# Forget-gate rows: repeated over the partitions by DMA from a scratch tensor in HBM, in place of GpSimd's broadcast

## The chip, the cores and the metric

The kernel runs on one core of one Trainium2 chip. The metric is the device time of one execution in microseconds (us), as a median of runs; less is better. The engines are TensorE (PE, matrix products; its weight loads are listed apart as PEld), VectorE (DVE), ScalarE (ACT), GpSimd (POOL) and SyncE (SP, which here only issues transfers). [...]

## The reference

Two layers of a decoder trunk work on 512 tokens of width 1024, in float32. Layer 0 splits its heads between differential attention (A) and forgetting attention (B), layer 1 uses dilated windows; each layer ends in a gated output projection and a per-layer embedding. What matters here is the forgetting attention. Each of its four heads has one gate logit per token, and the running sum of the logarithms of the gates' sigmoids is added to the scores, by query and by key:

```python
cum_logf = jnp.cumsum(jax.nn.log_sigmoid((f_logit + b_forget).astype(jnp.float32)), axis=1)
ob = fox_attention(qb, kb, vb.reshape(b, s_len, N_HEADS_B, HEAD_DIM), cum_logf)
...
s = jnp.einsum('bqhd,bkhd->bhqk', qb, k).astype(jnp.float32)
s = s + jnp.swapaxes(cqb, 1, 2)[..., None] - c_k[:, :, None, :]
pr = jax.nn.softmax(jnp.where(causal, s, -jnp.inf), axis=-1)
return jnp.einsum('bhqk,bkhd->bqhd', pr.astype(v.dtype), v)
```

With queries on the partitions and keys along the row, the term of the query is one number per partition, and the term of the key, c_k, is a row of 512 numbers that every one of the 128 partitions needs.

## The kernel before

The program is a list of chunks (add_chunk); a chunk is a block of weights of 1024 by 512 with its units, one unit per 128 tokens or 128 columns. Each float32 product is made of three products of split parts (mm3, L173 to L175): weights and activations are split into a high part (by ACT, L142 or L145) and a low part (by DVE, L143 or L146). Weights come in slices of 256 rows through three staging buffers named raw (prep_slices, L155, issued on SP); while one chunk runs, the slices of the next are loaded and split.

Attention is laid between the projection units: slot runs what was deferred, starts the attention steps that are due (attend), loads and splits weights, and then emits one projection unit. A head has four steps, one per 128 queries (head_steps): scores on PE, bias and row minimum on DVE (L445), exponential on ACT (L447), scaling by the reciprocal sum on POOL (L486), transposes on PE (L492) and the product with the values (L502), each stage a slot later. The order in which each engine then runs its instructions is set when the program is built, by a scheduler that simulates the engines; on the chip each engine and each queue follows its own list in order.

The forget gates are one unit of their own at the end of the second A chunk (f_unit). It puts the four heads' logits on partitions 0, 32, 64 and 96, takes the logarithms, and DVE's scan (L661) sums them along the tokens into the tile ck, of which these four partitions matter. Three slots later the columns of ck are transposed into cq, the term of the query. When a B head begins, POOL repeats that head's row of ck over all partitions, into a buffer of the pool t2, which has nine buffers in rotation:

```python
if i == 0:
    box["ck"] = t2()
    G.partition_broadcast(box["ck"], ck[32 * h:32 * h + 1, :])
bt = t2()
V.scalar_tensor_tensor(bt[:, :n], box["ck"][:, :n], cq[:, i, h:h + 1],
                       consts["causal"][:, off:512], op0=OP.subtract, op1=OP.add)
```

The four heads read it in their four steps (L465). After attention B come the gate units (z_units): DVE scales the projection (L705), ACT and DVE make the sigmoid (L688 to L692), DVE multiplies (L707), and POOL multiplies with the attention output (L709) before the result is split for the output projection (out_units, L719 to L738), whose first steps also build the mask of layer 1 on DVE (setup_c, L346 to L368).

Of the kernel before, what the change touches and what calls it, by code (L numbers as in the profile page):

```python
# [12 lines left out]
F32 = mybir.dt.float32  # L13
# [6 lines left out]
P = 128  # L20
# [5 lines left out]
BIG = 1e30  # L26
# [21 lines left out]
def trunk_kernel(  # L48
# [6 lines left out]
    nc = tc.nc  # L55
    V, A, G, T = nc.vector, nc.scalar, nc.gpsimd, nc.tensor

    cpool = ctx.enter_context(tc.tile_pool(name="cpool", bufs=1))
    sb = ctx.enter_context(tc.tile_pool(name="sb", bufs=1))
    psum = ctx.enter_context(tc.tile_pool(name="psum", bufs=1, space=bass.MemoryType.PSUM))  # L60

    cnt = [0]
# [28 lines left out]

    A.preload_act_table_set("natural_log_exp_and_others")

    # ---------------------------------------------------------------- inputs
    x2 = x[0]
    out2 = out[0]
    wie, wio = w_in_even[0], w_in_odd[0]
# [16 lines left out]
    rcol = const([P, NT], "rcol")  # L114
# [4 lines left out]
    gcols = const([P, 2, KS], "gcols")  # L119
    A.dma_start(out=gcols, in_=norm_g.rearrange("l (k q) -> q l k", q=P))  # L120

    # --------------------------------------------------------------- helpers
    def newton(y, ms, tmp):
        V.tensor_tensor(tmp, y, y, op=OP.mult)
        V.tensor_tensor(tmp, tmp, ms, op=OP.mult)
# [11 lines left out]
        return y  # L137

    def split(hi, lo, src, gain=None):
        """hi + lo = src (* gain, by partition), each exact in the tensor engine's one-pass type."""  # L140
        if gain is not None:
            A.activation(hi, src, AF.Copy, scale=gain)  # L142
            V.scalar_tensor_tensor(lo, src, gain, hi.bitcast(F32), op0=OP.mult, op1=OP.subtract)  # L143
            return
        A.activation(hi, src, AF.Copy)  # L145
        V.tensor_tensor(lo, src, hi.bitcast(F32), op=OP.subtract)  # L146
# [43 lines left out]
            mm3(ps, wh[:, k % 2, sl], wl[:, k % 2, sl], hi[:, k % 4, tok], lo[:, k % 4, tok],  # L190
                k == 0, k == KS - 1)

    # ---------------------------------------------------------- slot pipeline
    # A slot is one projection unit on the tensor engine plus what the deferred steps add to it.
    clock = [0]
    later = {}

# [13 lines left out]
            split(hi[:, :, t * P:(t + 1) * P], lo[:, :, t * P:(t + 1) * P], px)  # L211

    def row_scale(t0, t1):
        """rrow[:, token] = rcol of that token on every partition, by an exact product with the identity."""
        px = psX()
        for t in range(t0, t1):
            diag = t2((P, P))
            V.tensor_single_scalar(diag, ident, rcol[:, t:t + 1], op=OP.mult)
            T.matmul(px[:, t, :], onesd, diag, start=True, stop=True)
        A.activation(rrow[:, t0 * P:t1 * P].rearrange("p (t n) -> p t n", n=P), px[:, t0:t1, :], AF.Copy,  # L220
                     scale=float(P))

    def setup_a():
# [18 lines left out]
        for h in range(4):  # L242
            nc.sync.dma_start(out=bfc[32 * h:32 * h + 1, :], in_=b_forget[0:1, h:h + 1])

        # ------------------------------------------------------------- constants
        causal = const([P, 512], "causal")
        G.memset(causal, 0.0)
        G.affine_select(out=causal, in_=causal, pattern=[[-1, 512]], compare_op=OP.is_ge,
                        fill=BIG, base=384, channel_multiplier=1)
        # ------------------------------------------------------------ rope tables  # L250
        inv = np.exp((np.float32(-math.log(THETA)) * np.arange(16, dtype=np.float32)
                      / np.float32(16)).astype(np.float32)).astype(np.float32)
        posf = const([P, NT], "posf")
# [21 lines left out]
        for c in (c1, c2, c3):  # L275
            axpb(hsq, nn, -c, 0.0)
            gadd(ang, ang, hsq)
        # sin and cos of the reduced angle from those of its half, |half| <= pi / 2
        axpb(ang, ang, 0.5, 0.0)
        gmul(hsq, ang, ang)  # L280

        def series(first, last):
            """sum over n = first, first + 2, ..., last of (-1)^(n // 2) half^(n - first) / n!"""
            acc = t2((P, NT, 16))
            axpb(acc, hsq, (-1.0) ** (last // 2) / math.factorial(last), 0.0)
            for n in range(last - 2, first, -2):
                axpb(acc, acc, 1.0, (-1.0) ** (n // 2) / math.factorial(n))
                gmul(acc, acc, hsq)
            axpb(acc, acc, 1.0, 1.0)
            return acc  # L290
# [50 lines left out]
    def setup_c():  # L341
        causal = consts["causal"]
        biasc = sb.tile([P, 512], F32, tag="ckb", bufs=1, name="biasc")
        # d(p, c) = p + 384 - c ; multiplicity = [d <= 128] + [d % 4 == 0] + [d % 16 == 0]
        di = t2((P, 512), I32)
        G.iota(di, pattern=[[-1, 512]], base=384 + 512, channel_multiplier=1)  # L346
        mult = t2()
        tmi = t2((P, 512), I32)
        tmf = t2()
        V.tensor_single_scalar(tmi, di, 3, op=OP.bitwise_and)  # L350
        V.tensor_copy(tmf, tmi)
        V.tensor_single_scalar(mult, tmf, 0.0, op=OP.is_equal)
        tmi = t2((P, 512), I32)
        V.tensor_single_scalar(tmi, di, 15, op=OP.bitwise_and)
        tmf = t2()
        V.tensor_copy(tmf, tmi)
        V.scalar_tensor_tensor(mult, tmf, 0.0, mult, op0=OP.is_equal, op1=OP.add)
        tmf = t2()
        V.tensor_copy(tmf, di)
        V.scalar_tensor_tensor(mult, tmf, float(512 + 128), mult, op0=OP.is_le, op1=OP.add)  # L360
        # -ln(mult) for mult in 1..3, BIG where mult is 0 or d < 0
        V.tensor_single_scalar(biasc, mult, 2.0, op=OP.is_equal)
        V.tensor_single_scalar(biasc, biasc, -math.log(2.0), op=OP.mult)
        V.tensor_single_scalar(tmf, mult, 3.0, op=OP.is_equal)
        V.scalar_tensor_tensor(biasc, tmf, -math.log(3.0), biasc, op0=OP.mult, op1=OP.add)
        V.tensor_single_scalar(tmf, mult, 0.0, op=OP.is_equal)
        V.scalar_tensor_tensor(biasc, tmf, BIG, biasc, op0=OP.mult, op1=OP.add)
        V.tensor_tensor(biasc, biasc, causal, op=OP.add)  # L368

        consts["biasc"] = biasc  # L370

    # ------------------------------------------------------------- attention
    def qk_post(ps, qk, qk0, t, kind):
        """qk: hi and lo [P, 2(q/k), 2(head), 512], feature-major."""
        ng = 8 if kind == "a" else 4
        w = 512 // ng
        raw = t2()
# [5 lines left out]
        if kind != "b":  # L383
# [6 lines left out]
            for i in range(2):  # L390
# [6 lines left out]
                G.tensor_tensor(tt[:, 1, i, :, half:rot], v4[:, i, :, 0:half], tb(sg, half, rot), op=OP.mult)  # L397
                G.tensor_tensor(tt[:, 0, i, :, :], x12, tb(cg, 0, rot), op=OP.mult)
                G.tensor_tensor(x12, tt[:, 0, i, :, :], tt[:, 1, i, :, :], op=OP.add)
        # the projection still lacks the token's factor r: norm(r u) = r u (r^2 mean(u^2) + eps)^-1/2  # L400
        V.tensor_single_scalar(ss, ss, rcol2[:, t:t + 1], op=OP.mult)
        y = rstd_small(ss, 1.0 / w, ng)
        V.tensor_single_scalar(y, y, rcol[:, t:t + 1], op=OP.mult)
# [12 lines left out]

        defer(QLAG, finish)

    # steps waiting for their turn: (first slot, weight, first stage)
    queue = deque()  # L420
    credit = [0.0]

# [27 lines left out]
    def head_steps(kind, hh, qk, qk0, v, vcol, fin, first, extra=None):  # L450
        box = {}
# [4 lines left out]
        def step(i):  # L456
            n = P * (i + 1)
            off = 384 - P * i
            if kind == "b":
                ck, cq, h = extra  # L460
                if i == 0:
                    box["ck"] = t2()
                    G.partition_broadcast(box["ck"], ck[32 * h:32 * h + 1, :])
                bt = t2()
                V.scalar_tensor_tensor(bt[:, :n], box["ck"][:, :n], cq[:, i, h:h + 1],  # L465
                                       consts["causal"][:, off:512], op0=OP.subtract, op1=OP.add)
                bias = bt[:, :n]
            else:
                bias = consts["causal" if kind == "a" else "biasc"][:, off:512]
# [67 lines left out]
            cost = (i + 1) * (0.76 if kind == "a" else 0.55)  # L537
            queue.append((first[i], cost, lambda i=i: step(i)))

    # ------------------------------------------------------------- chunk code  # L540
    jobs = []

    def add_chunk(wap, ranges, nk, units, rate=0.0, layer=None):
# [90 lines left out]
    def f_unit(w):  # L634
        def u():
# [24 lines left out]
            ck = sb.tile([P, 512], F32, tag="ckb", bufs=1, name="ck")  # L660
            V.tensor_tensor_scan(ck, uu, xx, 0.0, op0=OP.mult, op1=OP.add)  # L661
            cq = const([P, NT, 4], "cq")
            st["ck"], st["cq"] = ck, cq

            def fin():
                px = psX()
# [16 lines left out]
        return hi, lo  # L683

    def sigmoid_of(z):
        """exp(log_sigmoid(z)), log_sigmoid(z) = min(z, 0) - ln(1 + exp(-|z|))."""
        e = t2()[:, :z.shape[-1]]
        A.activation(e, z, AF.Abs)  # L688
        A.activation(e, e, AF.Exp, scale=-1.0)
        A.activation(e, e, AF.Ln, bias=1.0)  # L690
        V.scalar_tensor_tensor(e, z, 0.0, e, op0=OP.min, op1=OP.subtract)  # L691
        A.activation(e, e, AF.Exp)  # L692
        return e
# [19 lines left out]
        return units  # L713

    def joined(act, j):
        """the float32 value that a pair of parts stands for"""
        hi, lo = act[j // 4]
        o = t2()
        G.tensor_tensor(o, hi[:, j % 4, :].bitcast(F32), lo[:, j % 4, :].bitcast(F32), op=OP.add)  # L719
        return o  # L720
# [47 lines left out]
        defer(1, tr)  # L768

    def ple(pp, w, t, a, b):  # L770
        """columns by tokens of the per-layer embedding (layer 0), tokens by columns (layer 1)"""
        wh, wl = w
        pT = st["pT"]
        sl = slice(t * P, (t + 1) * P)
        for k in range(2):
            ph, pl, vh, vl = pT[:, 0, k], pT[:, 1, k], wh[:, k], wl[:, k]
            if st["layer"] == 0:
                mm3(pp, vh[:, sl], vl[:, sl], ph[:, a:b], pl[:, a:b], k == 0, k == 1)
            else:
                mm3(pp, ph[:, sl], pl[:, sl], vh[:, a:b], vl[:, a:b], k == 0, k == 1)  # L780
# [5 lines left out]
    HALVES = ((0, 256), (256, 512))  # L786

    def gate0_units(c):
        """layer 0: feature-major, straight into the parts that layer 1 multiplies"""
        def units(w):  # L790
            wp_t, wp_f = prep_slices(w_ple[0], [(c * 512, 512)], 2)

# [62 lines left out]
        return e  # L855

    def gate1_units(c):
        """layer 1: token-major, straight into the rows of the result"""
        def units(w):
            wp_t, wp_f = prep_slices(w_ple[1], [(c * 512, 512)], 2)  # L860

# [30 lines left out]
    def qk_r(q0, k0, pr):  # L892
        return [(q0 + pr * 256, 256), (k0 + pr * 256, 256)]

    # layer 0
    RA = 2.7
    RB = 1.9
    RC = 2.2
# [37 lines left out]
            return units(w)  # L936
        return un

    # layer 1
    add_chunk(wio, [(2048, 512)], KS, reset(v_units("va")), layer=1)  # L940
    add_chunk(wio, qk_r(0, 1024, 0), KS, qk_units("c", (0, 1), "va", "oa"), RC, layer=1)
    add_chunk(wio, qk_r(0, 1024, 1), KS, qk_units("c", (2, 3), "va", "oa"), RC, layer=1)
# [37 lines left out]
```

## Time and profile before

| | |
|---|---|
| median of 3 runs | 721.02 us (720.91 to 721.56) |
| span of the profiled execution, first to last instruction | 719.0 us |
| its own time with the edges | not given by the page |
| busy: PE, DVE, ACT, POOL | 693.6, 450.2, 402.1, 204.0 us |
| mean granted clock of TensorE | 0.989 |
| read from HBM, written to HBM | 55.93 MB, 2.10 MB |

The page is one profiled execution. Its busy table tells which engine has no room; its windows give busy time and granted clock stretch by stretch; its timeline lists single instructions with the idle time in front of them and what ended it. An instruction's line can be that of a helper, and numbers of buffers are left out of the names (t, P, raw).

### The profile page before, as it was taken

The page shows a single profiled execution, that of the slowest core. Times are in us where ns is not written, and L with a number is a line of the kernel's source. Part 1 is how long each engine was busy: PE and PEld are TensorE (multiplying, and loading weights), DVE is VectorE, ACT ScalarE, POOL GpSimd, SP SyncE. Part 2 cuts the span into 40 slices and gives each one's busy share as a digit, 9 for nine tenths or more (in the row PEclk, how much of TensorE's full clock was granted, in tenths as well). Part 3 has the DMA queues.
Part 4 walks back from the last instruction along what each step waited for, and adds up shares of the span by engine and source line. Part 5 has one row for each costly group of instructions (what it writes and reads, how often), then busy time and mean ns, then how long its engine had stood idle before and what let it go on. Part 6 is the DMA issues. An engine that isn't in the chain of part 4 may idle for free.

```text
span 719.0 us, 9994 instructions
## 1 busy us (share of the span) xinstructions
PE 693.6 (96%) x3424; PEld 570.9 (79%) x3424; DVE 450.2 (63%) x1045; ACT 402.1 (56%) x849; POOL 204.0 (28%) x410
## 2 busy tenths in 40 slices
PE   6999999999988999699999999999999999999997
PEld 5887777777767788588888788888888888888886
DVE  3658768849785679764757456735577585655242
ACT  5737655637664786224757545846567686354220
POOL 3874331101011236610332034312244235600000
PEclk9999999999999999899999999999999999999999
DMA  8533140402040303133224213303033040333121
GB/s 261 139 89 117 30 119 0 118 1 87 31 118 0 118 1 118 30 117 118 72 75 147 68 51 118 94 26 118 0 118 111 9 117 11 108 118 118 59 72 45
DMA packets 45291, 58.68 MB, mean 82 GB/s; under 512 B 7992, under 2 KB 25912, under 8 KB 45240
## 3 DMA queue, kind: packets, MB, share of 16 engines
q1 hardware_dynamic: 43176, 58.03, 26.4%
q8 instruction: 27, 0.44, 0.2%
q10 hardware_dynamic: 2064, 0.01, 0.2%
q14 instruction: 24, 0.20, 0.1%
HBM read 55.93 MB, written 2.10 MB: 81 GB/s over the span
## 4 chain that ended last, share of the span: by engine, by line
PE 82%; DVE 9%; issue 3%; ACT 2%; DMA 2%; POOL 2%; SPq 0%; DVEq 0%; ACTq 0%
PE pu L175 10%; PE pu L174 10%; PE pu L173 10%; PE pu_g L173 4%; PE pu_g L174 4%; PE pu_g L175 4%; PE pu_v L173 4%; PE pu_v L174 4%; PE pu_v L175 4%; PE po L502 4%; PE pu_o L173 4%; PE pu_o L174 3%; PE pu_o L175 3%; PE ps L173 3%; PE ps L174 2%
## 5 line engine op out<-in xcount | busy, mean ns | idle before, releaser
L143 DVE SCALAR_TENSOR_TENSOR wl<-raw,gcols,wh 128x512 fp32r<-128x512 f32 x128 | 95.9, 782 | 27.0 <-ACT wh L142 26.7
L173 PE MATMUL pu<-wh,ar 128*128 128x512 f32 x256 | 101.7, 397 | 0.0
L174 PE MATMUL pu<-wl,ar 128*128 128x512 f32 x256 | 101.1, 395 | 0.0
L175 PE MATMUL pu<-wh,ar 128*128 128x512 f32 x256 | 100.8, 394 | 0.0
L142 ACT ACTIVATE wh<-raw,gcols 128x512 fp32r<-128x512 f32 x128 | 84.9, 721 | 21.5 <-DMA raw<-in_w_in_even_dram 14.2
L486 POOL TENSOR_SCALAR P<-P,sm 128x128 f32<-128x128 f32 (+3 forms) x48 | 30.6, 641 | 121.7 <-DVE sm L479 71.7
L447 ACT ACTIVATE P<-P,sm 128x128 f32<-128x128 f32 (+3 forms) x80 | 44.6, 559 | 34.7 <-DVE sm L445 33.0
L146 DVE TENSOR_TENSOR wl<-raw,wh 128x1024 fp32r<-128x1024 f32 x36 | 47.9, 1341 | 14.8 <-ACT wh L145 14.5
L173 PEld LDWEIGHTS pu<-wh,ar 128*128 128x128 f32 x256 | 48.1, 188 | 11.1 <-issue 1.3
L175 PEld LDWEIGHTS pu<-wh,ar 128*128 128x128 f32 x256 | 48.1, 188 | 9.9
L174 PEld LDWEIGHTS pu<-wl,ar 128*128 128x128 f32 x256 | 48.1, 188 | 9.5 <-issue 0.3
L173 PE MATMUL pu_o<-ar,wh 128*128 128x512 f32 x128 | 49.9, 401 | 5.8 <-ACT ar L145 5.8
L175 PE MATMUL pu<-ar,wl 128*128 128x512 f32 x136 | 54.7, 402 | 0.0
L174 PE MATMUL pu<-ar,wh 128*128 128x512 f32 x136 | 54.6, 402 | 0.0
L173 PE MATMUL pu<-ar,wh 128*128 128x512 f32 x136 | 54.2, 399 | 0.0
L175 PE MATMUL pu_v<-wh,ar 128*128 128x512 f32 x128 | 52.2, 409 | 0.0
L173 PE MATMUL pu_v<-wh,ar 128*128 128x512 f32 x128 | 51.3, 403 | 0.7 <-DVE t L691 0.7
L174 PE MATMUL pu_v<-wl,ar 128*128 128x512 f32 x128 | 51.5, 402 | 0.0
L145 ACT ACTIVATE ar<-t 128x512 fp32r<-128x512 f32 (+1 forms) x41 | 25.3, 618 | 46.7 <-POOL t L709 18.9
L174 PE MATMUL pu_o<-ar,wh 128*128 128x512 f32 x128 | 50.9, 398 | 0.0
L175 PE MATMUL pu_o<-ar,wl 128*128 128x512 f32 x128 | 50.5, 396 | 0.0
L145 ACT ACTIVATE wh<-raw 128x1024 fp32r<-128x1024 f32 x36 | 38.0, 1058 | 20.1 <-DMA raw<-in_w_ple_gate_dram 6.9
(236 smaller groups left out, 1628.3 us busy)
## 6 DMA issues: line engine op xcount, KB each, us to landing
raw<-in_w_in_even_dram SPq DMA_DIRECT2D x16, 512.0 KB, 5.0
raw<-in_w_in_even_dram SPq DMA_DIRECT2D x32, 256.0 KB, 3.3
raw<-in_w_ple_gate_dram SPq DMA_DIRECT2D x16, 512.0 KB, 4.3
raw<-in_w_in_odd_dram SPq DMA_DIRECT2D x16, 512.0 KB, 4.2
raw<-in_w_in_odd_dram SPq DMA_DIRECT2D x32, 256.0 KB, 3.1
raw<-in_w_out_even_dram SPq DMA_DIRECT2D x8, 512.0 KB, 4.3
raw<-in_w_out_odd_dram SPq DMA_DIRECT2D x8, 512.0 KB, 5.0
ar<-in_x_dram SPq DMA_DIRECT2D x8, 256.0 KB, 6.7
```

The source lines that it names most:

```text
L142: A.activation(hi, src, AF.Copy, scale=gain)
L143: V.scalar_tensor_tensor(lo, src, gain, hi.bitcast(F32), op0=OP.mult, op1=OP.subtract)
L145: A.activation(hi, src, AF.Copy)
L146: V.tensor_tensor(lo, src, hi.bitcast(F32), op=OP.subtract)
L173: T.matmul(ps, lh, rh, start=first, stop=False)
L174: T.matmul(ps, lh, rl, start=False, stop=False)
L175: T.matmul(ps, ll, rh, start=False, stop=last)
L447: A.activation(pt, pt, AF.Exp, bias=st_[:, 0:1], scale=-1.0, accum_out=st_[:, 1:2])
L486: G.tensor_scalar(p1, p1, s1[:, 2:3], 0.0, op0=OP.mult, op1=OP.add)
L502: T.matmul(po[:, i * P:(i + 1) * P], v[:, j, vcol:vcol + P], pt[:, j, :], start=(j == 0), stop=(j == i))
```

## The change

The tile ck is written once to a scratch tensor in HBM, four rows of 512, by a transfer on SP. Each B head then fills its t2 buffer with a transfer on SP that reads its row 128 times. POOL's broadcast is gone. The other hunks of the diff only remove comments, and lines move by one to three (L463 becomes L464, L155 becomes L156, L486 becomes L487, L709 becomes L712).

```diff
     sb = ctx.enter_context(tc.tile_pool(name="sb", bufs=1))
+    dram = ctx.enter_context(tc.tile_pool(name="dram", bufs=1, space=bass.MemoryType.DRAM))
...
                 if i == 0:
                     box["ck"] = t2()
-                    G.partition_broadcast(box["ck"], ck[32 * h:32 * h + 1, :])
+                    nc.sync.dma_start(out=box["ck"], in_=ck[h:h + 1, :].broadcast_to((P, 512)))
...
             cq = const([P, NT, 4], "cq")
-            st["ck"], st["cq"] = ck, cq
+            rows = dram.tile([4, 512], F32, name="ck_rows")
+            nc.sync.dma_start(out=rows, in_=ck[0:P:32, :])
+            st["ck"], st["cq"] = rows, cq
```

On SP, in the stretch where the B heads and the gate units run, the list of transfers before was this (raw is a staging buffer of weights, the number after it is the buffer's use):

```order
L155 DMA raw_2363<-in_w_in_even_dram 128x2x512
L155 DMA raw_2450<-in_w_in_even_dram 128x2x512
L155 DMA raw_2544<-in_w_in_even_dram 128x2x512
L155 DMA raw_2620<-in_w_in_even_dram 128x2x512
L155 DMA raw_2691<-in_w_in_even_dram 128x2x512
L155 DMA raw_2767<-in_w_out_even_dram 128x2x512
L155 DMA raw_2839<-in_w_out_even_dram 128x2x512
L155 DMA raw_2896<-in_w_out_even_dram 128x2x512
```

After the change the same stretch of SP's list holds the four repeating transfers (the numbers of uses are four higher):

```order
L156 DMA raw_2367<-in_w_in_even_dram 128x2x512
L156 DMA raw_2454<-in_w_in_even_dram 128x2x512
L464 DMA t_384_1981<-ck_rows 128x512
L464 DMA t_445_2241<-ck_rows 128x512
L156 DMA raw_2548<-in_w_in_even_dram 128x2x512
L156 DMA raw_2624<-in_w_in_even_dram 128x2x512
L156 DMA raw_2695<-in_w_in_even_dram 128x2x512
L156 DMA raw_2771<-in_w_out_even_dram 128x2x512
L464 DMA t_504_2518<-ck_rows 128x512
L156 DMA raw_2843<-in_w_out_even_dram 128x2x512
L464 DMA t_542_2685<-ck_rows 128x512
L156 DMA raw_2900<-in_w_out_even_dram 128x2x512
```

The first two stand one behind the other, after the last of the loads that came in a group; the third and the fourth stand on either side of one load of the output weights.

On POOL, from the first B head on, the list before had an extra instruction (ISA) ahead of each broadcast, and another ahead of the ordinary instruction that follows it:

```order
L483 TENSOR_SCALAR P_1745<-P_1745,sm_1757 128x512
L463 ISA
L463 ISA t_384_1977<-ck 128x512
L486 ISA
L486 TENSOR_SCALAR P_1981<-P_1981,sm_1984 128x128
L463 ISA
L463 ISA t_445_2237<-ck 128x512
L486 ISA
L486 TENSOR_SCALAR P_2066<-P_2066,sm_2071 128x256
```

After the change these rows read:

```order
L484 TENSOR_SCALAR P_1749<-P_1749,sm_1761 128x512
L487 TENSOR_SCALAR P_1985<-P_1985,sm_1988 128x128
L487 TENSOR_SCALAR P_2070<-P_2070,sm_2075 128x256
```

Six rows are gone here, and six more at the third and the fourth broadcast; the instructions that stay keep their order.

The write of the rows stands on SP between two earlier weight loads:

```order
L156 DMA raw_1764<-in_w_in_even_dram 128x2x256 x2
L665 DMA ck_rows<-ck 4x512
L156 DMA raw_1841<-in_w_in_even_dram 128x2x256 x2
```

Before, these two loads followed each other directly.

## Rows read from the trace of the kernel before

**Rows 1.** The page's busy table: busy us, share of the span, instructions.

```profile
PE 693.6 (96%) x3424; PEld 570.9 (79%) x3424; DVE 450.2 (63%) x1045; ACT 402.1 (56%) x849; POOL 204.0 (28%) x410
```

**Rows 2.** Timeline of PE, 200 to 300: start, us, instruction, [idle before, what ended it].

```profile
206.98 0.44 PE L173 MATMUL ps<-ar 128*128 128x384 f32 x1 [1.44 <-ACT ar L142]
208.23 0.41 PE L492 MATMUL px<-ident,P 128*128 128x128 f32 x2 [0.81 <-DVE sm L127]
...
232.56 0.47 PE L492 MATMUL px<-ident,P 128*128 128x128 f32 x2 [2.26 <-POOL P L486]
...
251.88 0.44 PE L174 MATMUL ps<-ar,ar 128*128 128x384 f32 x1 [1.54 <-DVE ar L143]
...
298.08 1.65 PE L173 MATMUL pu_o<-ar,wh 128*128 128x512 f32 x3 [5.80 <-ACT ar L145]
```

**Rows 3.** Timeline of POOL, 170 to 252.

```profile
175.25 1.37 POOL L463 PARTITION_BROADCAST t<-ck  x1 [5.81 <-DVE sm L124]
...
198.31 0.80 POOL L463 PARTITION_BROADCAST t<-ck  x1 [6.04 <-issue]
206.58 0.51 POOL L486 TENSOR_SCALAR P<-P,sm 128x256 f32<-128x256 f32 x1 [7.46 <-issue]
...
232.04 1.04 POOL L486 TENSOR_SCALAR P<-P,sm 128x256 f32<-128x256 f32 x2 [7.01 <-issue]
...
249.43 1.27 POOL L709 TENSOR_TENSOR t<-t,ar 128x512 f32<-128x512 f32 x1 [7.30 <-issue]
```

**Rows 4.** Timeline of DVE, 180 to 256.

```profile
183.55 0.34 DVE L465 SCALAR_TENSOR_TENSOR t<-t,cq,causal 128x128 f32<-128x128 f32 x1
...
189.82 0.68 DVE L382 TENSOR_REDUCE sm<-t 128x4 f32<-128x512 f32 x1
...
199.15 0.35 DVE L465 SCALAR_TENSOR_TENSOR t<-t,cq,causal 128x128 f32<-128x128 f32 x1 [4.49 <-POOL t L463]
...
219.08 0.42 DVE L445 CUSTOM_DVE_ANT_0 P<-ps,t 128x256 f32<-128x256 f32 x1 [1.22 <-PE ps L175]
...
225.07 0.75 DVE L465 SCALAR_TENSOR_TENSOR t<-t,cq,causal 128x128 f32<-128x128 f32 x2 [2.14 <-POOL t L463]
...
238.82 0.75 DVE L465 SCALAR_TENSOR_TENSOR t<-t,cq,causal 128x512 f32<-128x512 f32 x1
...
245.72 0.35 DVE L465 SCALAR_TENSOR_TENSOR t<-t,cq,causal 128x128 f32<-128x128 f32 x1
...
250.74 0.69 DVE L705 TENSOR_TENSOR t<-pu,rrow 128x512 f32<-128x512 f32 x1 [3.41 <-POOL t L709]
```

**Rows 5.** Timeline of SP's issues, at 178 and at 201.

```profile
178.04 0.37 SPq L155 DMA_DIRECT2D raw<-in_w_in_even_dram  x1
...
201.13 0.37 SPq L155 DMA_DIRECT2D raw<-in_w_in_even_dram  x1
```

**Rows 6.** Windows of 4 us, PE: length, busy (instructions), granted clock, DMA share, GB/s.

```profile
208.00:212.00 4.00, 3.60 (x13) 0.62 0.64 192
...
232.00:236.00 4.00, 3.44 (x11) 0.60 0.00 0
```

**Rows 7.** Window of 20 us: PE, PEld, DVE, ACT, POOL busy; clock, DMA, GB/s.

```profile
260.00:280.00 20.00, 20.00 (x108) 16.92 (x106) 17.50 (x33) 17.13 (x35) 10.67 (x9) 1.00 0.26 80
```

**Rows 8.** DVE's scan in its timeline; SP's waits, 100 to 180 (total, times, longest).

```profile
120.85 1.22 DVE L661 TENSOR_TENSOR_SCAN ck<-t,t 128x512 f32<-128x512 f32 x1
...
SPq L155 <- DVE sm L479: 32.6, 1, 32.6
```

**Rows 9.** DMA issues: count, KB each, median us from issue to landing.

```profile
raw<-in_w_in_even_dram SPq DMA_DIRECT2D x32, 256.0 KB, 3.3
...
t<-in_qn_c_dram SPq DMA_DIRECT2D x1, 64.0 KB, 5.5
```

**Rows 10.** Timelines: the last gate product on PE, and DVE's scaling of it.

```profile
270.82 0.39 PE L175 MATMUL pu<-ar,wl 128*128 128x512 f32 x1
...
274.96 0.68 DVE L705 TENSOR_TENSOR t<-pu,rrow 128x512 f32<-128x512 f32 x1
```

## Prediction

> **What bounds the kernel now.** I read the page's busy table first: TensorE (PE) is busy 693.6 of 719.0 us [rows 1]. A term counts only if it opens a gap on PE or takes clock away from it. Next the windows of 20 us: apart from the start and the end, PE's losses lie between 200 and 300 us. There I looked for PE's instructions with idle time in front. Four gaps, 1.44, 0.81, 2.26 and 1.54 us, sum to **6.05 us**; a fifth of 5.80 us stands at 298.08 [rows 2].
>
> The timeline of GpSimd (POOL) tells why. A broadcast works 0.80 to 1.37 us, but POOL sits idle in front of each of the four (5.81 us at the least, 6.04 at the most), and again 7.46, 7.01 and 7.30 us in front of the next ordinary POOL instruction behind the last three, with "issue" as the cause: nothing that the profile shows held it [rows 3]. Behind the first a longer wait on data covers this. So POOL switches its program over and back, a round of about 6 + 1 + 7 = 14 us. Its occupancy hurts nobody; the delay does, because POOL works in order.
>
> How it reaches PE, gap by gap. (1) DVE stands 4.49 us at 199.15 for the second broadcast [rows 4]. The weight splits behind it free their staging buffers late, SP issues the next weight load only at 201.13 [rows 5], ACT waits for that load with the query parts queued behind it, and PE pays 1.44 and 0.81. (2) The switch back holds the scaling of a probability tile (L486) until 232.04 [rows 3], and PE's transpose of it waits 2.26 us. (3) The last switch back holds L709 until 249.43 [rows 3], DVE stands 3.41 us at 250.74 [rows 4], and PE waits 1.54 us for a key part that DVE makes behind that.
>
> **What goes.** Four broadcasts and their eight switches. All of the 6.05 us should go, and a second thing with it: in 208 to 212 the granted clock is 0.62 of full and in 232 to 236 it is 0.60, each right behind a gap [rows 6]; in 260 to 280, where PE has no gap, it is 1.00 [rows 7]. [...] The work lost is (1 − 0.62) × 4 = 1.5 and (1 − 0.60) × 4 = 1.6 us, **3.1 us** together.
>
> **What comes: one write of 8 KB.** It sits on SP ahead of weight loads for which SP stands 32.6 us anyway, and waits for a scan that starts at 120.85 and lasts 1.22, within that time [rows 8]. Cost 0; that standing is its cover, and its first reader comes over 50 us later. f_unit's transposes of ck stay.
>
> **What comes: four repeating loads of 256 KB on SP.** Nothing in the trace reads one 2 KB row of HBM 128 times. The nearest rows are plain weight loads of 256 KB, 3.3 us from issue to landing, and a partition-repeating load of 64 KB at the crowded start, 5.5 us [rows 9]. I take 3.3, the row with the same bytes, and 5.5 as the upper bound; no lower bound is needed, for a faster load finds DVE not yet there. Each load waits for its buffer and its place in SP's queue, and what is queued behind waits too:
> - First: behind the weight load of 178.04 [rows 5], so issued at 178.4 and landed at 181.7 (183.9 by the bound). DVE wants it at 183.55 [rows 4]. Cost 0 to 0.4 on DVE.
> - Second: its buffer is free when the reduction at 189.82 ends, 190.5, so it lands at 193.8 to 196.0. DVE was there at 199.15 − 4.49 = 194.66: 0 to 1.3 us of standing in place of 4.49 [rows 4]. Queued behind it is the weight load of 201.13, which needs DVE's splits and comes some 3 to 4 us earlier with them.
> - Third: its buffer is free behind the score step of 219.08, so issue 219.5, landing 222.8 to 225.0. DVE was there at 225.07 − 2.14 = 222.93: 0 to 2.1 in place of 2.14 [rows 4]. At the bound nothing is won, but none of PE's gaps hangs on this one.
> - Fourth: behind the bias step of 238.82, which reads the same buffer until 239.6, so landing 242.9 to 245.1; wanted at 245.72 [rows 4]. Cost 0.
>
> So at neither bound do the loads cost PE anything; DVE, ACT and SP get earlier.
>
> **What is late next.** Everything meets again at 298.08: PE has done every product that doesn't need the last gated tile, and waits 5.80 us for it. POOL makes that tile behind two joins that wait for the mask code on DVE (setup_c), and DVE is busy 17.50 of 20 us in 260 to 280 [rows 7]. PE's gain reaches the end only as far as this chain moves too. DVE sheds 4.49 + 2.14 + 3.41 = 10.0 us of standing [rows 4], more than PE's 9.15, so I let the chain move as far as PE, and the fifth gap stays. It could shrink: the last gate product ends at 271.2 on PE and DVE takes it at 274.96 [rows 10], a backlog of 3.8 us that the stalls left.
>
> **Sum.** 6.05 + 3.1 = 9.15 us off the profiled execution. Its span is 719.0; its own total isn't shown, but the three runs' median, 721.02, is 2.0 us above the span, so I take 2.0 as what lies around it and subtract from 721.0: 711.9, forecast **712**.
>
> [...] Each half of a switch shows as its own wait, 6 in front and 7 behind [rows 3]. [...]
>
> **Rivals.**
> - *Larger (15%)*: the backlog of 3.8 us goes too, and the fifth gap shrinks from 5.80 to 2.0. 721.0 − 9.15 − 3.8 = 708.1. For it: DVE sheds more than PE. Against: DVE is near its full load from 260 on.
> - *The meeting point follows only half (14%)*: the fifth gap widens to some 10 us. 721.0 − 4.6 = 716.4. For it: DVE's 17.50 of 20.
> - *Half a switch (8%)*: the 7 us belong to the ordinary instructions; gaps 2 and 3 and the second clock drop stay (2.26 + 1.54 + 1.6 = 5.4). 721.0 − 3.75 = 717.3. Against: the listing of POOL loses the extra instruction ahead of L486 and L709 too.
> - *Nothing (4%)*: POOL's waits have another cause and remain, so the change doesn't do what it says: 721.
> - *Slower (9%)*: 128 readings of one row take far longer than a plain load, and DVE stands for them. Against today the second breaks even at 199.15 − 190.5 = 8.6 us, the third at 225.07 − 219.5 = 5.6, the fourth at 245.72 − 239.6 = 6.1. At 15 us a load they are late by 6.4, 9.4 and 8.9, 24.7 us of DVE; PE now pays 6.05 for DVE's 10.0, so 24.7 × 0.6 = 14.8, less the 9.15: 721.0 + 5.7 = 727. It decides from about 12 us a load (15.7 late, 9.4 paid). No row of these sizes is beyond 5.5 us.
>
> **Chances and range.** Forecast 50%, rivals as above. Under 0.2% (1.4 us) a measurement can't tell a difference from none. Faster: 50 + 15 + 14 + 8 = 87%; same 4%; slower 9%. The range leaves out the last two and the far end of the larger case: 706.5 to 719.0, with the forecast's own from 710 to 714.
>
> **What would show it.** Right: no work of line 463 on POOL and no "issue" of 6 or 7 us there; the repeating loads land 3 to 5.5 us after issue; DVE waits for none of them above 2 us; PE loses none of the first four gaps, at a clock of 1.00 from 200 to 280. Wrong: a load landing after 6 us or more; SP standing at a repeating load while the weight load behind it is already wanted; a fifth gap clearly beyond 5.80 us (the half case) or near 2 (the larger); new gaps on PE for parts that come from ACT.

## The result and the profile after

The changed kernel takes **709.28 us** (median of 4 runs, 708.33 to 709.8), the kernel before, on the same chip, 721.29 (4 runs, 720.91 to 723.31). The ratio is 0.9836, with a 95% interval of 0.9822 to 0.985: 12.0 us less, where 9.15 were forecast. The time lies inside the stated range of 706.5 to 719.0, below the 710 to 714 that the forecast gave itself. The span of the profiled execution falls from 719.0 to 707.9 us, by 11.1.

The page's busy table and its chain of work (shares of the span by engine), after the change; the first line answers to [rows 1]:

```profile
PE 689.8 (97%) x3424; PEld 569.5 (80%) x3424; DVE 451.6 (64%) x1045; ACT 403.2 (57%) x849; POOL 201.7 (28%) x406
...
PE 92%; DVE 3%; DMA 2%; ACT 1%; POOL 1%; issue 1%; SPq 0%; DVEq 0%; ACTq 0%
```

With the same 3424 instructions PE is busy 3.8 us less, and idle 18.1 us in place of 25.4, which is 7.3 less. The two make up the 11.1.

PE's gaps of more than 0.3 us from 200 to 300, after; the first is new, the second is what is left of [rows 2]:

```profile
208.77 0.50 PE L174 MATMUL pu<-ar,wh 128*128 128x512 f32 x1 [0.44 <-ACT t L381]
...
285.84 1.65 PE L174 MATMUL pu_o<-ar,wh 128*128 128x512 f32 x3 [4.29 <-ACT ar L146]
```

The four gaps are gone. The fifth has shrunk from 5.80 to 4.29 us, and stands 12.24 us earlier.

Windows of 20 us, after (length, busy us of PE, PEld, DVE, ACT, POOL with instructions; granted clock, DMA share, GB/s), answering to [rows 6, 7]:

```profile
200.00:220.00 20.00, 19.56 (x107) 16.55 (x106) 14.29 (x44) 12.83 (x33) 2.53 (x4) 1.00 0.32 101
220.00:240.00 20.00, 20.00 (x106) 16.87 (x105) 18.28 (x45) 15.15 (x33) 5.17 (x6) 1.00 0.38 115
240.00:260.00 20.00, 20.00 (x115) 17.37 (x114) 16.16 (x36) 17.80 (x36) 7.37 (x7) 1.00 0.06 14
260.00:280.00 20.00, 20.00 (x110) 17.15 (x108) 19.69 (x28) 9.41 (x19) 13.75 (x10) 1.00 0.31 97
280.00:300.00 20.00, 15.71 (x64) 12.58 (x64) 14.01 (x14) 6.38 (x9) 9.32 (x6) 0.83 0.20 64
```

From 200 to 280 PE loses 0.44 us and runs at a granted clock of 1.00 throughout: the two clock drops have gone with the gaps in front of them. The one behind the fifth gap is still there (0.83).

The repeating loads in SP's issues (start, us, the issuing instructions) and in the list of DMA issues (count, KB each, median us from issue to landing), and DVE's first reads of the first two:

```profile
178.72 13.86 SPq L464 DMA_DIRECT2D t<-ck_rows  x2
197.39 4.54 SPq L156 DMA_DIRECT2D raw<-in_w_in_even_dram  x3
...
216.47 0.34 SPq L464 DMA_DIRECT2D t<-ck_rows  x1
...
231.50 0.34 SPq L464 DMA_DIRECT2D t<-ck_rows  x1
```

```profile
t<-ck_rows SPq DMA_DIRECT2D x4, 256.0 KB, 3.1
```

```profile
184.32 0.35 DVE L466 SCALAR_TENSOR_TENSOR t<-t,cq,causal 128x128 f32<-128x128 f32 x1 [0.39 <-DMA t<-ck_rows]
...
195.34 0.35 DVE L466 SCALAR_TENSOR_TENSOR t<-t,cq,causal 128x128 f32<-128x128 f32 x1 [0.71 <-DMA t<-ck_rows]
```

Here a row repeated 128 times takes about as long as a plain load of the same bytes, 3.3 us [rows 9]: three loads took 3.1 us and the first, behind the weight loads, 5.6. DVE stands 1.5 us for three of them, where it stood 6.6 for the broadcasts, and the weight load that SP issued at 201.13 [rows 5] now goes out at 197.39.

What the prediction calls a switch has a name in the trace before. The extra instructions in POOL's list show up as MODIFY_POOL_CONFIG, two records ahead of each broadcast (engine, instruction, count: ns at the least, median and most, first and last start):

```profile
L463 POOLq MODIFY_POOL_CONFIG  x8: 1/8/11, 169.4 to 235.2; - x8
```

Eight more stand ahead of the ordinary instruction behind each broadcast (six on L486, two on L709). Each records at most 0.13 us of its own; the broadcast starts 5.6 to 5.9 us behind the first of its pair, and the ordinary instruction, where it waits for no data, 7.1 to 7.5 behind the first of its own. In the trace after, both kinds are gone from this stretch. That they stand for a change of program is the author's reading; what the trace shows is these records and the waits with them.

### The profile page after: what moved, and what is told of

It is laid out like the page before. It is cut to its first block, busy times and chain, and to the rows that moved or that the text cites. A ratio compares the mean times of both kernels' runs of the same rounds, so it can differ in the third digit from the quotient of the medians.

```text
span 707.9 us, 9982 instructions
## 1 busy us (share of the span) xinstructions
PE 689.8 (97%) x3424; PEld 569.5 (80%) x3424; DVE 451.6 (64%) x1045; ACT 403.2 (57%) x849; POOL 201.7 (28%) x406
## 4 chain that ended last, share of the span: by engine, by line
PE 92%; DVE 3%; DMA 2%; ACT 1%; POOL 1%; issue 1%; SPq 0%; DVEq 0%; ACTq 0%
PE pu L176 12%; PE pu L174 12%; PE pu L175 12%; PE po L503 5%; PE pu_g L176 4%; PE pu_g L174 4%; PE pu_g L175 4%; PE pu_v L174 4%; PE pu_v L175 4%; PE pu_v L176 4%; PE pu_o L174 4%; PE pu_o L175 4%; PE pu_o L176 4%; PE ps L174 3%; PE ps L175 2%; PE ps L176 2%
## 5 line engine op out<-in xcount | busy, mean ns | idle before, releaser
L487 POOL TENSOR_SCALAR P<-P,sm 128x128 f32<-128x128 f32 (+3 forms) x48 | 30.9, 647 | 132.9 <-DVE sm L480 98.3
L174 PEld LDWEIGHTS pu<-wh,ar 128*128 128x128 f32 x256 | 48.1, 188 | 11.1 <-issue 1.3
L147 DVE TENSOR_TENSOR wl<-raw,wh 128x1024 fp32r<-128x1024 f32 x36 | 47.8, 1339 | 14.2 <-ACT wh L146 13.7
```

The costliest lines, as they stand in the source:

```text
L174: T.matmul(ps, lh, rh, start=first, stop=False)
L487: G.tensor_scalar(p1, p1, s1[:, 2:3], 0.0, op0=OP.mult, op1=OP.add)
```

## The experiments

Three theories stood at the start. **A**: the switch holds up whatever stands behind it in POOL's order. **B**: only the broadcast's late data mattered, DVE's waits for it. **C**: the gain is the scheduler's, which orders the program anew. It does so: PE, DVE and ACT run parts of this stretch in another order after the change, and on POOL one scaling (L487, of 384 columns, at about 262) has moved ahead of two joins, so that POOL's instructions keep their order only around the broadcasts. Each run is compared with the kernel before on the same chip; diffs are against the changed kernel unless it is said otherwise.

### Half of the heads back on POOL

```diff
-                    nc.sync.dma_start(out=box["ck"], in_=ck[h:h + 1, :].broadcast_to((P, 512)))
+                    if h < 2:
+                        G.partition_broadcast(box["ck"], st["ck_sb"][32 * h:32 * h + 1, :])
+                    else:
+                        nc.sync.dma_start(out=box["ck"], in_=ck[h:h + 1, :].broadcast_to((P, 512)))
```

> The changed kernel, with heads 0 and 1 repeated by POOL's broadcast as before and heads 2 and 3 by DMA. Theory A: gap 1 (1.44 + 0.81 us) and the first drop of the clock (1.7) come back, the other two don't: about 713.3 us (712 to 715), and POOL shows two rounds of 6 + 1 + 7 us. Together with the run for heads 2 and 3 the losses against the changed kernel add up to what the change won, 9 to 12 us. Theory C: the loss has no relation to which heads POOL serves; 709 or 721.

Measured: 711.67 us (710.78 to 713.18), ratio 0.9876 (0.985 to 0.9902), 2.4 us above the changed kernel. The same with the condition turned round (h >= 2):

> The changed kernel, with heads 2 and 3 repeated by POOL's broadcast and heads 0 and 1 by DMA. Theory A: gaps 2 and 3 (2.26 + 1.54 us) and the second drop of the clock (1.7) come back, 5.5 us, and the gap before the output product is as wide as before: about 715 us (713 to 718). Theory C: 709 or 721, whichever heads it is.

Measured: 717.94 us (716.91 to 719.24), ratio 0.9955 (0.9941 to 0.997), 8.7 us above. POOL's timeline with heads 2 and 3 on it, and PE's two gaps:

```profile
219.40 0.80 POOL L465 PARTITION_BROADCAST t<-ck  x1 [5.82 <-PE ps L176]
227.37 1.03 POOL L490 TENSOR_SCALAR P<-P,sm 128x256 f32<-128x256 f32 x2 [7.17 <-issue]
...
236.36 1.12 POOL L465 PARTITION_BROADCAST t<-ck  x1 [6.02 <-DVE sm L446]
245.67 1.25 POOL L716 TENSOR_TENSOR t<-t,ar 128x512 f32<-128x512 f32 x1 [8.20 <-issue]
```

```profile
227.89 0.44 PE L496 MATMUL px<-ident,P 128*128 128x128 f32 x2 [2.73 <-POOL P L490]
...
248.09 0.69 PE L175 MATMUL ps<-ar,ar 128*128 128x384 f32 x1 [4.00 <-DVE ar L144]
```

Each half brings back its own two gaps: with heads 0 and 1 they are 0.93 and 0.81 us and the clock stays at 1.00, with heads 2 and 3 they are these, and the window from 240 to 260 shows a clock of 0.91. The run with heads 0 and 1 lies just under its 712 to 715, since the clock drop that was expected with its gaps didn't come; the other lies in its range, with the fifth gap at 5.47 us. The two losses, 2.4 and 8.7, sum to 11.1 of the 12.0 won. So the gain belongs to the single broadcasts where they stand, which speaks against C, and most of it to the last two, where an ordinary instruction that PE soon needs (L490, L716) stands behind the switch back.

### A broadcast that nobody reads

A and B part where the broadcast stays on POOL and nothing reads what it writes.

```diff
                     nc.sync.dma_start(out=box["ck"], in_=ck[h:h + 1, :].broadcast_to((P, 512)))
+                    G.partition_broadcast(st["idle"], st["ck_sb"][32 * h:32 * h + 1, 0:448])
```

> The changed kernel, and on POOL, where a head begins, a broadcast of 448 of the row's 512 columns into a tile that nobody reads. So POOL switches its program there and back four times as before, but DVE gets its rows by DMA. Theory A (the switch holds up whatever stands behind it in POOL's order, and that reaches PE): the scalings and products behind the last two switches are late by 7 us again, gaps 2 and 3 of the kernel before and one drop of the clock come back, 5.4 us: about 714.7 us (712.5 to 717). Theory B (only the late broadcast's data mattered, DVE's waits of 4.5 and 2.1 us): nobody waits for it now, 709 to 710.5. Theory C (the gain comes from the new order that the scheduler gave the engines, POOL's instructions don't matter): 709 to 710.

Measured: 709.55 us (708.18 to 710.08), ratio 0.9847 (0.9819 to 0.9874), no loss. This did not settle it. POOL's timeline shows why:

```profile
125.10 3.22 POOL L465 PARTITION_BROADCAST idle<-ck  x4 [5.51 <-DVE sm L481]
135.54 0.47 POOL L485 TENSOR_SCALAR P<-P,sm 128x256 f32<-128x256 f32 x1 [7.22 <-ACT ar L610]
```

As nothing ties them to a head, all four went to 125, right behind the scan, in one batch where POOL had nothing urgent. What the run does show is that four broadcasts in one batch (0.74 us each) cost no time there, and needed one switch over and one back. The next run takes the row from the tile that the load has just filled, so that the broadcast can't come before its head:

```diff
+                    G.partition_broadcast(st["idle"], box["ck"][0:1, 0:448])
```

> The kernel after, and each head also has POOL broadcast 448 columns from the row that the load has just repeated, into a tile that nobody reads; since it reads the head's own tile it can't be drawn ahead to a quiet stretch, as the unread broadcast of the earlier run could. DVE still takes the bias from the load. Theory A (a switch of POOL's program holds up whatever stands behind it in POOL's order): the waits of 6 and 7 us come back on POOL at the heads, the scaling of the probability tile (L487) and the gate's multiply (L712) are late again, PE has gaps at about 228 and 248 as with heads 2 and 3 by POOL, and a clock drop with them; the first two gaps, which began at DVE's wait for the second broadcast's data, stay away: 714 to 717.5. Theory B (only the data of the broadcast came late): POOL's waits come back but cost nothing, 709 to 710.5.

Measured: **724.41 us** (723.64 to 725.53), ratio 1.0038 (1.0026 to 1.005), 15.1 us above the changed kernel. POOL's timeline:

```profile
199.38 1.26 POOL L465 PARTITION_BROADCAST idle<-t  x1 [6.04 <-issue]
208.56 0.57 POOL L488 TENSOR_SCALAR P<-P,sm 128x384 f32<-128x384 f32 x1 [7.91 <-DVE t L467]
...
242.41 2.21 POOL L465 PARTITION_BROADCAST idle<-t  x1 [9.07 <-DMA t<-ck_rows]
252.51 1.25 POOL L714 TENSOR_TENSOR t<-t,ar 128x512 f32<-128x512 f32 x1 [7.89 <-issue]
```

DVE, and PE's gaps:

```profile
253.79 0.69 DVE L710 TENSOR_TENSOR t<-pu,rrow 128x512 f32<-128x512 f32 x1 [7.39 <-POOL t L714]
```

```profile
235.29 1.12 PE L411 MATMUL px<-ident,t 128*128 128x128 f32 x4 [4.43 <-ACT pt L496]
...
255.18 1.12 PE L411 MATMUL px<-ident,t 128*128 128x128 f32 x4 [6.67 <-DVE t L406]
```

B falls: DVE has its data from the loads, and the time is lost all the same (DVE's waits from 170 to 300: us in all, times, longest):

```profile
DVE t L467 <- DMA t<-ck_rows: 2.1, 3, 0.7
```

C falls as well. PE, DVE, ACT and SP run the same instructions in the same order in the trace of this run and in that of the changed kernel (3424, 1045 and 849 instructions, 179 transfers); POOL's list differs by the four broadcasts and their switches alone. Nothing waits for a broadcast's result, and ACT, which feeds PE, stands 10.24 and 8.34 us for L714 behind the third and the fourth switch back (until 232.69 and 253.79). A holds: the first two gaps stay away, the later ones return, though the loss is larger than the 4.7 to 8.2 us expected. The fourth broadcast waits here for its own load, so the switch back ends at 252.51 where before the change it ended at 249.43 [rows 3]; L714 is late by that, DVE stands 7.39 us behind it, and PE 6.67.

### The rows repeated by TensorE

If leaving POOL is all that counts, another engine should do as well. The edit is against the kernel before:

```diff
-                    G.partition_broadcast(box["ck"], ck[32 * h:32 * h + 1, :])
+                    px = psX().rearrange("p a b -> p (a b)")
+                    T.matmul(px, ident[:, 32 * h:32 * h + 1].to_broadcast([P, P]), ck, start=True, stop=True)
+                    A.activation(box["ck"], px, AF.Copy)
```

> The kernel before, with the rows repeated by a third way: PE multiplies ck with a column of the identity repeated 128 times, and ACT copies the result to the same t2 buffer. Neither POOL nor HBM takes part. Theory A (what counts is that POOL doesn't switch): as the changed kernel, plus four products in float32 of 512 columns on PE, 0.86 us each: 709.3 + 3.4 = 712.7 us (711 to 714.5). Rival (the gain belongs to the way over SP and HBM, or to the order that the scheduler made around it): no gain, 719 to 724.

Measured: 721.89 us (720.58 to 722.09), ratio 1.0002 (0.999 to 1.0015). The expectation missed; the time lies in the rival's range, so by itself it would speak for the way over SP and HBM or for the order. The trace gives another reason. POOL's long waits before L488 now name data as their cause, but the waits of DVE from 170 to 300 (us in all, times, longest) read:

```profile
DVE t L467 <- ACT t L465: 9.2, 3, 6.8
```

ACT's copy stands in ACT's own order, behind a product that stands in PE's; DVE gets the row up to 6.8 us late, worse than from POOL (6.6 in all), and PE pays again (2.63 us at 240.43, 5.06 at 299.36); the four products took 1.0 to 1.1 us each, as the like product at L520 does in the trace before (1.02 in PE's timeline, 0.86 along the chain). Of the three ways tried, only the DMA does both: it leaves POOL's order, and it enters that of no engine that computes. SP's order it does enter, which the next run tests.

### Twice the loads

```diff
-                    nc.sync.dma_start(out=box["ck"], in_=ck[h:h + 1, :].broadcast_to((P, 512)))
+                    for _ in range(2):
+                        nc.sync.dma_start(out=box["ck"], in_=ck[h:h + 1, :].broadcast_to((P, 512)))
```

> The changed kernel, each head's row loaded twice into the same buffer, so the second load waits on SP until the first has landed (3.1 us) and the row comes 3.1 us or more later. It measures how much room the loads have. Theory A with the prediction's bounds: DVE stands some 3 to 4 us for heads 1 and 2 in place of 0.4 to 0.7, less than the 8.6 us at which head 1 would be as late as before; PE loses 0 to 2 us: 709.3 to 711.5. Rival (the loads are just in time, every microsecond of delay reaches PE): 4 x 3.1 = 12 us of DVE, 713 us and more.

Measured: 710.32 us (709.02 to 711.12), ratio 0.9853 (0.9828 to 0.9879). DVE stands 8.6 us for the loads in place of 1.5, and PE pays 0.99 in place of 0.44 at the same instruction. The fifth gap is 5.82 us in place of 4.29:

```profile
287.56 1.65 PE L174 MATMUL pu_o<-ar,wh 128*128 128x512 f32 x3 [5.82 <-ACT ar L146]
```

Seven more microseconds of standing on DVE go with 1.0 us of time, and the two intervals overlap: SP and DVE have room for these transfers, though not without limit, and the rival of loads that are just in time was far off. The scheduler also ordered this program anew, so how much of the fifth gap is the loads' stays open.

### The fifth gap

What is left is the gap in front of the output projection. Three rows of the trace after show who is last: in ACT's timeline the copy of the last attention output, in POOL's the joins and the last gate multiply.

```profile
280.25 0.60 ACT L509 ACTIVATE ar<-po 128x512 f32<-128x512 f32 x1 [5.33 <-PE po L503]
```

```profile
280.47 3.44 POOL L722 TENSOR_TENSOR t<-ar,ar 128x512 f32<-128x512 f32 x2 [2.22 <-DVE t L367]
283.87 1.26 POOL L712 TENSOR_TENSOR t<-t,ar 128x512 f32<-128x512 f32 x1
```

L712 has its data at 280.85 and runs at 283.87, behind two joins that waited for the mask code (L367). In the trace before, the same rows are:

```profile
289.15 0.60 ACT L508 ACTIVATE ar<-po 128x512 f32<-128x512 f32 x1 [4.37 <-PE po L502]
```

```profile
292.71 3.44 POOL L719 TENSOR_TENSOR t<-ar,ar 128x512 f32<-128x512 f32 x2 [2.22 <-DVE t L366]
296.11 1.26 POOL L709 TENSOR_TENSOR t<-t,ar 128x512 f32<-128x512 f32 x1
```

There it was held from 289.75 to 296.11. One version builds the mask (setup_c) one slot after the gates' columns, long before:

```diff
+                defer(1, setup_c)
...
-                if l == 0 and j == 2:
-                    setup_c()
```

> The changed kernel, with the mask code of layer 1 (setup_c) emitted one slot after cq is made instead of in the third output unit. That is open only after the change, since the mask shares ck's buffer, which POOL read until the last broadcast. Theory A (what is left before the output product, a gap of 4.29 us and 4.9 us at half clock behind it, is set by the mask code on DVE): both go, 4.3 + 2.4 = 6.7 us: about 702.6 us (701 to 705). Rival (that gap is set by the chain of the last gated tile itself, or by POOL's load): 707 to 709. Third (the mask code holds up DVE where the first B heads begin and opens new gaps): 710 and more.

Measured: 708.16 us (707.83 to 709.48), ratio 0.9815 (0.9788 to 0.9841). The expectation missed: the time lies in the rival's range, and its interval overlaps that of the changed kernel, so no gain is shown. DVE is free, but now PE waits 1.07 us at 277.51 and 2.25 at 286.36, where the last multiply waits for ACT's copy, and the mask code on DVE from 142.68 to 157.16 goes with small gaps of 0.58, 0.42 and 0.30 on PE at 163 to 182. The other goes the opposite way, to the seventh output unit:

```diff
-                if l == 0 and j == 2:
+                if l == 0 and j == 6:
                     setup_c()
```

> The kernel after, with the mask of layer 1 (setup_c) built in the seventh output unit instead of the third, so that DVE's 14 instructions of it (268.7 to 282.8) leave the stretch ahead of the fifth gap. Theory M (the fifth gap is what is left of a chain in which POOL's joins wait for buffers that the mask code holds, and the last gate multiplies stand behind the joins): the gap goes from 4.29 to under 1.5 us and the half clock behind it with it, 702 to 705. Rival N (the joins then wait for other buffers of the same pool, and the multiply behind them as long): gap of 3 to 6 us, 707 to 710.

Measured: **704.58 us** (703.99 to 704.86), ratio 0.9762 (0.9749 to 0.9774), clear of the changed kernel's interval. PE, POOL and a window of 4 us of this run:

```profile
282.17 0.98 PE L174 MATMUL pu_o<-ar,wh 128*128 128x512 f32 x3 [1.36 <-ACT ar L146]
```

```profile
280.19 1.26 POOL L712 TENSOR_TENSOR t<-t,ar 128x512 f32<-128x512 f32 x1 [3.93 <-ACT ar L509]
```

```profile
284.00:288.00 4.00, 4.00 (x19) 3.09 (x18) 4.00 (x8) 3.31 (x5) 0.43 (x1) 1.00 0.01 3
```

The joins fill the buffers first, and the mask code (15 instructions on DVE) comes behind; its first one waits for a buffer that the last multiply reads:

```profile
281.48 0.43 DVE L351 TENSOR_SCALAR t<-t 128x512 int32<-128x512 int32 x1 [5.86 <-POOL t L712]
```

The last multiply waits for ACT's copy alone, the gap is 1.36 us and the clock stays at 1.00. This beats both kernels. Two more runs move the joins into the buffers of the probability tiles, alone and with the late mask:

```diff
-        o = t2()
+        o = sb.tile([P, 512], F32, tag="P", bufs=PBUFS, name=nm("t"))
```

> The kernel after, with the joins of the output units (L722) in the buffers of the probability tiles, five of them and nearly idle by then, instead of the nine of t2; the mask code stays where it is. Theory M: the joins don't wait for the mask code any more, so the last two multiplies come as soon as DVE's product is there (about 272): fifth gap under 1.5 us, 702 to 705. Rival N2 (DVE itself is late there, by its own order: its split of the last gated tile stands behind the mask code): the gap stays within 1 us of 4.29, 708 to 710.

Measured: 707.82 us (707.27 to 708.09), ratio 0.9807 (0.9794 to 0.9819).

> Both edits together: joins in the probability buffers and the mask code four units later. If the joins' buffers alone are the cause, as with the joins alone (702 to 705); if DVE's order is it too, 701 to 704 here and 708 to 710 with the joins alone; if neither, 707 to 710.

Measured: 708.4 us (707.04 to 708.72), ratio 0.9812 (0.98 to 0.9825). Both miss 702 to 705, although PE's gap at the last tile is 1.36 us in both. The window of 20 us with both edits:

```profile
260.00:280.00 20.00, 17.46 (x88) 14.26 (x88) 19.86 (x29) 8.57 (x18) 12.92 (x10) 0.97 0.26 83
```

With buffers free, the mask code starts on DVE at 267.37 although it is emitted four units later, and DVE's split of an earlier gated tile stands among it: PE waits 1.90 us at 278.56 (<- DVE ar L147), as it does with the joins' buffers alone at 279.20. So the held buffers and DVE's order are both part of the cause; the late mask alone works because there the joins, filling t2, keep the mask code back until 281.48. The last run gives the kernel before the late mask alone:

> The kernel before, POOL's broadcasts kept, with the mask of layer 1 built in the seventh output unit. If the fifth gap has the same cause before the change (the last gate multiply, whose data ACT has at 289.75, stands on POOL until 296.11 behind joins that wait for the mask code), the gap goes from 5.80 to about 1.4 us and part of the half clock behind it too: 714.5 to 717, and the two edits add up (12.0 and 4.7 won apart and together). If before the change the chain was late for the broadcasts' sake, the gap stays above 4 us: 719.5 to 721.5.

Measured: 718.38 us (717.29 to 719.18), ratio 0.9947 (0.993 to 0.9963). The fifth gap falls from 5.80 to 2.26 us, and POOL's last gate multiply now waits for ACT's copy, so its cause is the same before the change, though less is won than the 5 to 7 us expected: the clock still drops behind the gap (0.92 in 280 to 300), it drops once more behind the fourth gap (0.91 in 240 to 260, where before the change it was 1.00), and the four gaps are 1.37, 0.59, 2.95 and 1.87, 0.7 us more in all. The change wins 12.0, the late mask 3.6, and both together 17.1 (721.65 − 704.58).

## Why the prediction was right, and by how much it was off

**POOL's switch and the four gaps.** Right. No broadcast and no switch is left on POOL in this stretch, its waits there end with data but for one of 3.3 us ("issue"), and the 6.05 us are gone less 0.44 of a new gap: 5.6. That the switch delays what stands behind it in POOL's order, and that this reaches PE, is shown by the unread broadcast in place. The third rival, by which the 7 us belong to the ordinary instructions, falls with it: they carry a MODIFY_POOL_CONFIG of their own only behind a broadcast, and L487 and L712 have no such wait after the change. The wait in front is 5.82 and 6.02 us with heads 2 and 3 on POOL, as before the change (5.81 to 6.04 [rows 3]); each broadcast paid it anew there, and four in one batch paid it once (5.51 us). The wait behind is 7.17 and 8.20 us with heads 2 and 3. The broadcast is the shorter instruction (0.80 to 1.37 against 3.1 us), and the kernel is faster without it (709 against 721 us), for the waits that go with it are longer.

**The clock.** Right for the two drops: the clock is 1.00 from 200 to 280. The 3.1 us were read from windows of 4 us, which hold idle time and cut off the end of each drop. Where the two traces record the granted clock, it is either 1.00 or 0.50, the lower level: products of the output projection start every 0.43 us at 0.50 (287.29 to 290.28, after) and every 0.23 at 1.00 (from 291.03). At 0.50 are the stretches 208.94 to 212.36 and 232.84 to 236.25, with 3.25 and 3.41 us of PE's work in them, half of which is 3.3 us.

**The write and the loads.** The write goes out at 122.16 and holds nothing back: SP's next weight load follows at 133.22, before the change at 133.16. For the loads, right: 3.1 and 5.6 us, a little outside 3.3 and 5.5 on either side, issued at 178.7, 192.2, 216.5 and 231.5 against 178.4, 190.5, 219.5 and 239.6 (the later ones are earlier because everything is). No term was needed for them: before the fifth gap PE pays 0.44 us in all, as much as they can have cost there.

**The step that was off: "I let the chain move as far as PE, and the fifth gap stays."** PE stops in front of that gap 10.73 us earlier (292.28 before, 281.55 after), but DVE's mask code, which takes the same 11.3 us in both traces from its first instruction to the one that the joins wait for, starts 12.26 us earlier (280.95 and 268.69). The gap shrinks by the difference, 1.5 us. DVE was further ahead because its backlog went in part: it takes the last gate product 1.2 us after PE ends it (261.51 and 262.74), before 3.8 [rows 10].

```profile
261.12 0.39 PE L176 MATMUL pu<-ar,wl 128*128 128x512 f32 x1
...
262.74 0.67 DVE L708 TENSOR_TENSOR t<-pu,rrow 128x512 f32<-128x512 f32 x1
...
268.69 0.41 DVE L351 TENSOR_SCALAR t<-t 128x512 int32<-128x512 int32 x1
```

That is the mechanism of the rival *Larger*, at 1.5 of its 3.8 us. The other runs that build the mask in the third unit line up with it: the backlog is 4.7 us with the loads doubled, 2.4 with heads 2 and 3 on POOL, 1.9 with the broadcast in place and 1.3 with heads 0 and 1, and the fifth gap is 5.82, 5.47, 4.98 and 4.39. The clock took 1.0 of it back: behind the gap PE works 5.0 us at the lower level where it worked 3.0.

```profile
284.00:288.00 4.00, 2.16 (x5) 1.66 (x6) 1.20 (x1) 0.63 (x1) 2.40 (x2) 0.51 0.14 55
288.00:292.00 4.00, 4.00 (x13) 3.11 (x13) 3.29 (x6) 2.20 (x4) 0.54 (x1) 0.64 0.00 0
```

These two windows of the trace after cost 0.49 × 2.16 + 0.36 × 4 = 2.5 us. Before, in the gap and behind it, they were

```profile
294.00:298.00 4.00, 0.00 (x0) 0.00 (x0) 1.02 (x1) 0.60 (x1) 3.92 (x4) 0.53 0.30 109
298.00:302.00 4.00, 3.92 (x11) 3.06 (x12) 2.51 (x4) 0.66 (x2) 0.71 (x1) 0.61 0.00 0
```

and cost 0.39 × 3.92 = 1.5.

**The account of the span.** 5.6 (four gaps) + 3.3 (two clock drops) + 1.5 (fifth gap) − 1.0 (the clock behind it) = 9.4, and 0.4 for a gap of 0.38 at 280.45 that went as well. Of the 11.1 us this leaves 1.3, PE's busy time over equal counts of instructions in the main; no row assigns it, and its cause stays open. The clock at the kernel's end has no part in it: it falls at 717.5 before and at 707.3 after, when PE has done its last product. The medians differ by 12.0 and the spans by 11.1, and that is the choice of executions: the one profiled after the change took 709.72 us, 0.4 above its median, with 1.8 us outside the span. With as much outside it, the one before took about 720.8 (an estimate), 0.5 below its median. So of the 2.85 us by which the forecast was short, the step named above gave 0.5, clock included, the choice of executions 0.9, and 1.3 is not explained.

## What to carry to other kernels

Price an instruction that comes with a MODIFY_POOL_CONFIG on POOL by what stands behind it in POOL's order, not by its own duration: here 0.8 us of work held its neighbours up for 14, and it cost nothing where four of them were batched in a quiet place. A replacement should not enter the order of an engine that is itself waited for; here a DMA into a buffer that was free in time was the cheapest of the three ways tried (709.28 us, against 721.29 by POOL and 721.89 by PE and ACT). And where two chains meet, work out the shift of each one apart: the shorter gap was worth 1.5 us here, and the helper work that stood in it (a mask not needed for long) was worth 4.7 more.

## What was not expected of the hardware

Between the two profiled executions the shorter gap cost more clock: 3.0 us of work at the lower level behind the gap of 5.80 us, 5.0 behind the one of 4.29. The stretch at the lower level is as long in both, 6.8 us: it runs from 294.3 to 301.1 before and from 284.1 to 290.9 after. What differs is how much of it falls into the gap, where PE has no work to lose: 3.8 us before, 1.8 after.

This is no rule of the gap's length. With the loads doubled a gap of 5.82 us was followed by 4.7 us at the lower level (0.83 in 280 to 300), and the gaps of 4.40 (unread broadcasts in one batch) and 4.39 us (heads 0 and 1 on POOL) by 3.4 (0.91 in both). A gap of 1.90 us was followed by a drop with both edits (0.97 in 260 to 280, 0.95 in 280 to 300) and by none with the joins' buffers alone (1.00 in both windows); the 1.36 us of the late mask left the clock at 1.00. So the 1.0 us that the clock took back is the luck of these two executions, and a difference of that size between two kernels may be the clock alone.

A MODIFY_POOL_CONFIG does not cost 6 us by itself. At the start of both kernels POOL runs two MODIFY_POOL_CONFIG as well (1.5 to 1.8 us), and there the next instruction starts within 0.1 us. What makes the difference, no run shows.

POOL's switch back is not one number: it was 7.01 to 7.46 us before [rows 3], 6.75 with heads 0 and 1 on POOL, and 7.17 to 8.20 with heads 2 and 3.
